# A hybrid DeltaNet and S5 layer: where the S5 output units stand, and when their loads are issued

## The chip, the cores and the metric

The kernel runs on one core of a Trainium2 chip. The core has TensorE (PE, with its weight loads PEld), VectorE (DVE), ScalarE (ACT), GpSimd (POOL) and SyncE (SP), each of which works through its own list of instructions in order, and 16 DMA engines that they share. The metric is the device time of one execution in microseconds, the median over runs.

## The reference

One layer of a streaming encoder, for a prompt of 4096 frames and a running stream of 32 frames, each of width 1024. Cut to what matters:

```
h = rms_norm(x) ;  p = h @ w_in             # q,k,v | a,b | z_dn | u_s5 | z_s5
q,k,v = silu(causal_conv4(p_qkv)) ;  o_dn = gated_delta_rule(q, k, v, g, beta)   # 4 heads of 128
o_dn = rms_norm(o_dn) * silu(z_dn)
y = Re(C x_t) + D u_t ;  x_t = Lbar x_{t-1} + Bbar u_t                           # S5, 32 groups of 16
gy = gelu(y)
o_s5 = gy * sigmoid(gy @ glu_w + glu_b) * silu(z_s5)                             # 512 x 512 matmul
out = rms_norm(x + concat(o_dn, o_s5) @ w_out)
```

The caches and the states at the end are returned too. The frames are independent in all but the convolution, the delta rule (in chunks) and the S5 scan.

## The kernel before, in words

The program is built with a planner: each operation becomes an instruction with a priority (the place at which it was written, unless a priority is given), and the planner sets the order of every engine's list by times that it reckons itself. An engine then keeps to its list; a wait at its head holds all that is behind it. `after(inst, mark)` adds an order between two instructions.

**Phase A** (to some 920 us) does the norm, the projections of u and z, the S5 scan, and the decay tables. `gy = gelu(y)` is left in DRAM as `gy_d`, `silu(z_s5)` as `z5_d`. The largest value of the S5 output is reduced over the partitions by POOL (`allmax`, tile `am_g`); `pow2` (lines 150 to 155, three small DVE instructions) makes of it the power of two `e_gy` by which gy is scaled, and `scales` (L1055) makes the further scales `gs`, `mm`, `hdn`, `ss5` from that. `table(ci)` (L1039) makes one of 33 decay tables: four matmuls into `pt`, one DVE addition into `tdm` (three buffers), four exponentials on ACT, one store to `dm_d`.

**Phase B** interleaves five streams of work in `Drive.run`, which keeps a reckoned time of PE's work: four streams of delta-rule chunks (33 chunks of 128 frames, the sample's among them) go first when they are ready, and the stream `dense` (L1179) fills in between. `dense` does, for each block b of 256 frames, the q, k, v projection (`qkv`, 288 matmuls of 259 columns) and then two **S5 units**. From b = 2 on it first waits until the chunks of block b - 2 have passed their front part. A unit, `s5out(k, j)` (L1435), takes 128 frames of the S5 output: it loads a tile of gy (256 KB, into `gyt`, two buffers) and of z (`zr`, two buffers) by the SP queue, splits gy into two halves `gh` (one buffer; ACT, then DVE, both at line L222 and L223 of a helper), transposes it (four PE instructions, L52), multiplies by the glu weights (12 matmuls of 512 columns, at L48, `pp<-wg,gh`), and finishes by DVE, ACT, DVE, ACT and POOL (L1462 to L1473); the result lies in the buffer of `zr` and is stored by the POOL queue (L1475). There are 32 units of the prompt and one of the sample, (-1, 0). With `LATE = 8`, blocks 1 to 12 are followed by two units each, blocks 13 to 15 by none, and eight units come at the end, behind `c_weights` (L1798), which loads `w_out` through one buffer `xw` in four parts and splits it into `wo`. The units share a ring of three PSUM tiles `pp` with `qkv`.

**Phase C** is `out` (L1820), the output projection of 16 blocks and of the sample; the first seven are the last part of `dense`.

The lines that the change touches most:

```
units = units[:len(units) - LATE]
for b in list(range(1, SP)) + [-1] + list(range(SP, NB)):
    if b > 1:
        yield lambda: {2 * b - 4, 2 * b - 3} <= self.front
    yield from self.qkv(b) if b >= 0 else self.qkv_s()
    for u in units[:2] if b >= 0 else [(-1, 0)]:
        yield from self.s5out(*u)
```

Of the kernel before, what the change touches and what calls it, by code (L numbers as in the profile page):

```python
# [11 lines left out]
ALU = mybir.AluOpType  # L12
# [5 lines left out]
H = 4  # L18
# [3 lines left out]
TS = 32  # L22
# [6 lines left out]
SB = 2  # L29
Z0 = 3  # L30
KS = 4096.0
LATE = 8
SLACK = 1.5


# [44 lines left out]
class Trunk:  # L80
# [168 lines left out]
    def phase_a(self):  # L249
        nc, io = self.nc, self.io  # L250
# [97 lines left out]
        v = nc.vector  # L348
# [3 lines left out]
        v.tensor_single_scalar(mx, mx, 91.0, op=ALU.add)  # L352
        ma = self.allmax(mx, 1, "g")
        self.e_gy = cst.tile([128, 2], F32, name="e_gy")
        self.pow2(ma, self.e_gy[:, 0:1], self.e_gy[:, 1:2])
        self.right.close()
        self.tbl = self.pool(bld, "b_tbl", 3)
        self.pt = self.pool(bld, "b_pt", 2, psum=True)
# [5 lines left out]
        with self.tc.high_priority(offset=-250):  # L364
            for ci in order:
                self.table(ci)

        gcf = self.ngC.rearrange("t h c -> t (h c)")
        mark = self.last_exp
# [669 lines left out]
    def table(self, ci):  # L1039

        nc = self.nc
        gc, c, n = (self.gcr["p"], ci, self.NC) if ci < self.NC else (self.gcr["s"], 0, 1)
        ps = self.pt.tile([128, H, 128], F32, name="pt")
        k = H * n
        for h in range(H):
            p = h * n + c
            nc.tensor.matmul(ps[:, h], self.ident[:k, p:p + 1].to_broadcast([k, 128]), gc, start=True, stop=True)  # L1047
        dm = self.tbl.tile([128, H, 128], F32, name="tdm")
        nc.vector.tensor_tensor(dm, ps, self.low.unsqueeze(1).to_broadcast([128, H, 128]), op=ALU.add)
        for h in range(H):  # L1050
            self.last_exp = nc.scalar.activation(dm[:, h], dm[:, h], AF.Exp, bias=self.ngC[:, h, ci:ci + 1])
            self.after(self.last_exp, self.last_gelu)
        nc.scalar.dma_start(self.dm_d[ci], dm)
# [93 lines left out]
    def phase_b(self):  # L1147
# [30 lines left out]

        def dense():  # L1179
            units = [(k, j) for k in range(NB // 4) for j in range(8)]  # L1180
            late = units[len(units) - LATE:]
            units = units[:len(units) - LATE]
            for b in list(range(1, SP)) + [-1] + list(range(SP, NB)):
                if b > 1:
                    yield lambda: {2 * b - 4, 2 * b - 3} <= self.front
                yield from self.qkv(b) if b >= 0 else self.qkv_s()
                for u in units[:2] if b >= 0 else [(-1, 0)]:
                    yield from self.s5out(*u)
                if b >= 0:
                    units = units[2:]  # L1190
# [206 lines left out]
    def qkv_s(self):  # L1397
# [34 lines left out]
            self.blk[-1, nm] = dst[:, H * i:H * i + H]  # L1432
        yield 0

    def s5out(self, k, j):  # L1435


# [4 lines left out]
        gy, zr, gh = self.rm["gyt"][:, at], self.rm["zr"][:, at], self.rm["gh"][:, 0]  # L1442
        t, m5 = gy, zr
        gy = gy.rearrange("p (o i) -> p o i", o=4)[:, :, :m]
        if k >= 0:
            nc.sync.dma_start(gy, self.gy_d[k].rearrange("o c t -> c o t")[:, :, 128 * j:128 * j + 128])
        else:

            nc.sync.dma_start(gy, self.gys_d.rearrange("o c t -> c o t"))
            g = gh.rearrange("p (o i) -> p o i", o=4)[:, :, :m]  # L1450
            gp.tensor_copy(g.rearrange("p o (i s) -> p o s i", s=8), gy.rearrange("p o (s i) -> p o s i", s=8))
            gp.tensor_copy(gy, g)
        rows = (lambda d: d.rearrange("(i s) d -> s i d", s=8)[j]) if k >= 0 else (lambda d: d)
        nc.sync.dma_start(zr[:m], rows(self.z5_d[k] if k >= 0 else self.z5s_d))
        gh = gh.bitcast(F16).rearrange("p (x o i) -> p x o i", x=2, o=4)[:, :, :, :m]
        self.split(gh[:, 0], gh[:, 1], gy, self.gs)
        pt = self.pb.tile([128, 512], F32, name="pp")[:m]
# [15 lines left out]
        gp.tensor_tensor(m5[:, 1], t, m5[:, 0], op=ALU.subtract)  # L1473
        dst = self.m5_d[k].rearrange("x (i s) d -> x s i d", s=8)[:, j] if k >= 0 else self.m5s_d
        gp.dma_start(dst.rearrange("x t d -> t x d"), m5)  # L1475

    def load_be(self, ci):

# [471 lines left out]
```

## Time and profile before

| what | us |
|---|---|
| median of 3 runs | 2348.45 (2343.35 to 2357.0) |
| the profiled execution, its own time | 2354.65 |
| its span, first to last instruction | 2352.8 |
| PE busy | 2068.0 (88%) |
| DVE / ACT / POOL busy | 1440.2 / 1251.0 / 959.4 |

The span is what the trace covers; the profiled execution's own time is 1.85 us above it, and lies 6.2 us above the median of the runs. Engines work side by side, so their busy times don't add up; a stage is as long as the list of that engine on which the others wait.

### The profile page before, as it was taken

The page shows a single profiled execution, that of the slowest core. Times are in us where ns is not written, and L with a number is a line of the kernel's source. Part 1 is how long each engine was busy: PE and PEld are TensorE (multiplying, and loading weights), DVE is VectorE, ACT ScalarE, POOL GpSimd, SP SyncE. Part 2 cuts the span into 40 slices and gives each one's busy share as a digit, 9 for nine tenths or more (in the row PEclk, how much of TensorE's full clock was granted, in tenths as well). Part 3 has the DMA queues.
Part 4 walks back from the last instruction along what each step waited for, and adds up shares of the span by engine and source line. Part 5 has one row for each costly group of instructions (what it writes and reads, how often), then busy time and mean ns, then how long its engine had stood idle before and what let it go on. Part 6 is the DMA issues. An engine that isn't in the chain of part 4 may idle for free.

```text
span 2352.8 us, 47799 instructions
## 1 busy us (share of the span) xinstructions
PE 2068.0 (88%) x18304; PEld 1492.9 (63%) x18304; DVE 1440.2 (61%) x3289; ACT 1251.0 (53%) x3695; POOL 959.4 (41%) x1444
## 2 busy tenths in 40 slices
PE   4688889888699998698799999989899868999998
PEld 3354677665467554487787778777778755554443
DVE  4685577559466222387687787778777786642223
ACT  5357546543386121376776677667677775431110
POOL 1344225212301012355666666666666675420000
PEclk9899899999899999799899999999999989999999
DMA  6169957765993644323133333322232145455542
GB/s 196 66 175 243 212 116 193 156 54 116 186 235 91 125 114 114 64 59 78 38 79 82 66 80 81 80 62 50 74 82 56 55 146 129 130 165 155 141 139 93
DMA packets 426349, 269.21 MB, mean 114 GB/s; under 512 B 344476, under 2 KB 379384, under 8 KB 425608
## 3 DMA queue, kind: packets, MB, share of 16 engines
q1 hardware_dynamic: 399400, 189.82, 37.1%
q0 software_dynamic: 21968, 67.69, 10.3%
q10 hardware_dynamic: 4752, 8.65, 1.2%
q8 instruction: 143, 2.34, 0.4%
q14 instruction: 86, 0.70, 0.1%
HBM read 102.27 MB, written 86.09 MB: 80 GB/s over the span
## 4 chain that ended last, share of the span: by engine, by line
PE 43%; issue 11%; ACT 7%; DMA 7%; DVE 6%; POOL 4%; SPq 1%; DVEq 0%; POOLq 0%; ACTq 0%
PE pp L48 23%; PE pz L522 9%; PE bk L48 7%; DMA gyt<-gy_d 3%; PE bk L52 2%; DVE acc L1384 2%; ACT jk L1555 2%; DMA dm_d<-tdm 1%; PE pt L1047 1%; DMA hz<-h_d 1%; DVE kn L1667 1%; DMA ab_d<-abt 1%; SPq L1349 1%; ACT acc L1382 1%; ACT br L1642 1%
## 5 line engine op out<-in xcount | busy, mean ns | idle before, releaser
L522 PE MATMUL pz<-wz,hz 128*128 128x512 f16 (+1 forms) x1464 | 385.7, 389 | 27.6 <-DMA hz<-h_d 25.5
L1384 DVE SCALAR_TENSOR_TENSOR acc<-pp,cwu,acc 128x256 f32<-128x256 f32 x540 | 252.9, 477 | 67.4 <-ACT acc L1382 60.6
L48 PEld LDWEIGHTS <-mx 128*128 128x128 f16 (+1 forms) x1584 | 152.3, 98 | 177.2 <-issue 1.6
L522 PEld LDWEIGHTS <-hz 128*128 128x128 f16 (+1 forms) x1464 | 143.4, 99 | 187.3 <-DMA hz<-h_d 33.3
L48 PE MATMUL pp<-h,wk 128*128 128x259 f16 (+1 forms) x1632 | 222.7, 276 | 0.1
L530 PE MATMUL pp<-wa,ht 128*128 128x260 f16 x1536 | 196.3, 284 | 27.1 <-ACT wa L222 10.4
L48 PE MATMUL pp<-h,wq 128*128 128x259 f16 (+1 forms) x1632 | 214.6, 273 | 0.5 <-DVE acc L1384 0.5
L48 PE MATMUL pp<-h,wv 128*128 128x259 f16 (+1 forms) x1632 | 209.9, 272 | 1.0 <-DVE acc L1384 1.0
L48 PE MATMUL po<-wo,mx 128*128 128x512 f16 (+1 forms) x912 | 197.2, 379 | 0.3 <-ACT acc L1219 0.3
L530 PEld LDWEIGHTS <-ht 128*128 128x128 f16 x1536 | 153.7, 101 | 57.1 <-issue 23.9
L48 PEld LDWEIGHTS <-wk 128*128 128x128 f16 x1632 | 156.5, 100 | 35.9 <-issue 8.8
L48 PEld LDWEIGHTS <-wq 128*128 128x128 f16 x1632 | 152.4, 99 | 27.6 <-issue 5.5
L48 PEld LDWEIGHTS <-wv 128*128 128x128 f16 x1632 | 148.5, 98 | 22.6 <-issue 1.6
L48 PE MATMUL pp<-wo,mx 128*128 128x512 f16 x672 | 152.0, 379 | 0.0
L556 POOL DMA_DIRECT2D z_d<-zt x64 | 36.8, 576 | 260.2 <-DVE zt L555 217.4
L1845 ACT ACTIVATE junk<-xt 128x1024 bf16<-128x1024 f32 (+1 forms) x19 | 20.1, 1056 | 176.4 <-issue 92.6
L48 PE MATMUL pp<-wg,gh 128*128 128x512 f16 (+1 forms) x396 | 104.2, 391 | 6.4 <-ACT gh L222 3.4
L555 DVE SCALAR_TENSOR_TENSOR zt<-zt,pz 128x512 f32<-128x512 f32 (+1 forms) x66 | 44.9, 680 | 102.0 <-ACT zt L554 101.3
L1382 ACT ACTIVATE acc<-pp,cwu 128x256 f32<-128x256 f32 x180 | 84.8, 482 | 38.6 <-PE pp L48 38.0
L48 PEld LDWEIGHTS <-a 128*128 128x128 f16 x1320 | 78.2, 98 | 37.3 <-issue 28.3
L1844 DVE SCALAR_TENSOR_TENSOR xt<-po,uo,xt 128x512 f32<-128x512 f32 (+1 forms) x38 | 28.5, 749 | 116.7 <-PE po L48 116.6
L948 POOL DMA_DIRECT2D gy_d<-vv x128 | 67.7, 535 | 78.7 <-ACT vv L943 40.3
(615 smaller groups left out, 5011.1 us busy)
## 6 DMA issues: line engine op xcount, KB each, us to landing
xn<-in_x SPq DMA_DIRECT2D x32, 512.0 KB, 4.5
h_d<-hl POOLq DMA_DIRECT2D x32, 512.0 KB, 5.4
z_d<-zt POOLq DMA_DIRECT2D x64, 256.0 KB, 3.6
xt<-in_x SPq DMA_DIRECT2D x18, 512.0 KB, 4.3
out_y<-xt SPq DMA_DIRECT2D x18, 512.0 KB, 3.6
dm_d<-tdm ACTq DMA_DIRECT2D x33, 256.0 KB, 3.7
dm<-dm_d SPq DMA_DIRECT2D x33, 256.0 KB, 2.9
gy_d<-vv POOLq DMA_DIRECT2D x128, 64.0 KB, 3.9
```

The source lines that it names most:

```text
L48: return self.nc.tensor.matmul(out, lhs, rhs, start=start, stop=stop)
L52: return self.nc.tensor.transpose(out, src, ident)
L522: self.nc.tensor.matmul(ps, a[x][:, c], w[:, y, c], start=c == 0 and x == y == 0, stop=c == K - 1 and x == 1)
L530: self.nc.tensor.matmul(pu[hf][:, :260], ht[x][:, c, :m], self.w_a[:, y, c, 260 * hf:260 * hf + 260], start=c == 0 and x == y == 0, stop=c ...
L555: nc.vector.scalar_tensor_tensor(zt, zt, 1.0, pz, op0=ALU.add, op1=ALU.mult)
L556: nc.gpsimd.dma_start(rows(dst[0][blk]) if blk >= 0 else dst[1], zt)
L948: gp.dma_start(gy[s], gn[16 * s:16 * s + 16, :, :128])
L1047: nc.tensor.matmul(ps[:, h], self.ident[:k, p:p + 1].to_broadcast([k, 128]), gc, start=True, stop=True)
L1382: nc.scalar.activation(acc, ps[:, 0:n], AF.Copy, scale=cw[:, e, 0:1])
L1384: v.scalar_tensor_tensor(acc, ps[:, j:j + n], cw[:, e, j:j + 1], acc, op0=ALU.mult, op1=ALU.add)
L1555: act.activation(junk, src[:, h], AF.Square, accum_out=out[:, h:h + 1])
L1844: v.scalar_tensor_tensor(xt[:m, sl], ps, self.uo[:m], xt[:m, sl], op0=ALU.mult, op1=ALU.add)
```

## The change

It has three parts. `pow2` of the S5 bound, and with it all that is made from it, is written behind the tables, and its first instruction is ordered behind the last table's DVE addition. Of the units, four (`EARLY`) are written between the sample's unit and the wait ahead of block 2, and four instead of eight stay for the end; blocks 1 to 12 keep two each. And the loads move: the first four units (self.nu counts them from 1) load for themselves on SP as before; from the third unit on, each unit ends by issuing the loads of the unit after the next, which uses the same buffers: gy on the POOL queue, behind the unit's own store, and z on the SP queue, where it must wait until that store has landed.

```diff
--- before.py
+++ after.py
@@ -29,7 +29,8 @@
 SB = 2
 Z0 = 3
 KS = 4096.0
-LATE = 8
+LATE = 4
+EARLY = 4
 SLACK = 1.5


@@ -352,7 +353,6 @@
         v.tensor_single_scalar(mx, mx, 91.0, op=ALU.add)
         ma = self.allmax(mx, 1, "g")
         self.e_gy = cst.tile([128, 2], F32, name="e_gy")
-        self.pow2(ma, self.e_gy[:, 0:1], self.e_gy[:, 1:2])
         self.right.close()
         self.tbl = self.pool(bld, "b_tbl", 3)
         self.pt = self.pool(bld, "b_pt", 2, psum=True)
@@ -364,6 +364,8 @@
         with self.tc.high_priority(offset=-250):
             for ci in order:
                 self.table(ci)
+        self.after(v.tensor_single_scalar(ma, ma, 2.0 ** -100, op=ALU.max), self.last_tdm)
+        self.pow2(ma, self.e_gy[:, 0:1], self.e_gy[:, 1:2])

         gcf = self.ngC.rearrange("t h c -> t (h c)")
         mark = self.last_exp
@@ -1046,7 +1048,7 @@
             p = h * n + c
             nc.tensor.matmul(ps[:, h], self.ident[:k, p:p + 1].to_broadcast([k, 128]), gc, start=True, stop=True)
         dm = self.tbl.tile([128, H, 128], F32, name="tdm")
-        nc.vector.tensor_tensor(dm, ps, self.low.unsqueeze(1).to_broadcast([128, H, 128]), op=ALU.add)
+        self.last_tdm = nc.vector.tensor_tensor(dm, ps, self.low.unsqueeze(1).to_broadcast([128, H, 128]), op=ALU.add)
         for h in range(H):
             self.last_exp = nc.scalar.activation(dm[:, h], dm[:, h], AF.Exp, bias=self.ngC[:, h, ci:ci + 1])
             self.after(self.last_exp, self.last_gelu)
@@ -1178,9 +1180,14 @@

         def dense():
             units = [(k, j) for k in range(NB // 4) for j in range(8)]
+            self.useq = units[:2] + [(-1, 0)] + units[2:]
             late = units[len(units) - LATE:]
             units = units[:len(units) - LATE]
             for b in list(range(1, SP)) + [-1] + list(range(SP, NB)):
+                if b == 2:
+                    for u in units[:EARLY]:
+                        yield from self.s5out(*u)
+                    units = units[EARLY:]
                 if b > 1:
                     yield lambda: {2 * b - 4, 2 * b - 3} <= self.front
                 yield from self.qkv(b) if b >= 0 else self.qkv_s()
@@ -1432,6 +1439,14 @@
             self.blk[-1, nm] = dst[:, H * i:H * i + H]
         yield 0

+    def s5load(self, k, j, at, eng):
+        m = 128 if k >= 0 else TS
+        gy = self.rm["gyt"][:, at].rearrange("p (o i) -> p o i", o=4)[:, :, :m]
+        eng.dma_start(gy, self.gy_d[k].rearrange("o c t -> c o t")[:, :, 128 * j:128 * j + 128] if k >= 0 else
+                      self.gys_d.rearrange("o c t -> c o t"))
+        rows = (lambda d: d.rearrange("(i s) d -> s i d", s=8)[j]) if k >= 0 else (lambda d: d)
+        self.nc.sync.dma_start(self.rm["zr"][:m, at], rows(self.z5_d[k] if k >= 0 else self.z5s_d))
+
     def s5out(self, k, j):


@@ -1442,16 +1457,13 @@
         gy, zr, gh = self.rm["gyt"][:, at], self.rm["zr"][:, at], self.rm["gh"][:, 0]
         t, m5 = gy, zr
         gy = gy.rearrange("p (o i) -> p o i", o=4)[:, :, :m]
-        if k >= 0:
-            nc.sync.dma_start(gy, self.gy_d[k].rearrange("o c t -> c o t")[:, :, 128 * j:128 * j + 128])
-        else:
-
-            nc.sync.dma_start(gy, self.gys_d.rearrange("o c t -> c o t"))
+        if self.nu <= 4:
+            self.s5load(k, j, at, nc.sync)
+        if k < 0:
+
             g = gh.rearrange("p (o i) -> p o i", o=4)[:, :, :m]
             gp.tensor_copy(g.rearrange("p o (i s) -> p o s i", s=8), gy.rearrange("p o (s i) -> p o s i", s=8))
             gp.tensor_copy(gy, g)
-        rows = (lambda d: d.rearrange("(i s) d -> s i d", s=8)[j]) if k >= 0 else (lambda d: d)
-        nc.sync.dma_start(zr[:m], rows(self.z5_d[k] if k >= 0 else self.z5s_d))
         gh = gh.bitcast(F16).rearrange("p (x o i) -> p x o i", x=2, o=4)[:, :, :, :m]
         self.split(gh[:, 0], gh[:, 1], gy, self.gs)
         pt = self.pb.tile([128, 512], F32, name="pp")[:m]
@@ -1473,6 +1485,8 @@
         gp.tensor_tensor(m5[:, 1], t, m5[:, 0], op=ALU.subtract)
         dst = self.m5_d[k].rearrange("x (i s) d -> x s i d", s=8)[:, j] if k >= 0 else self.m5s_d
         gp.dma_start(dst.rearrange("x t d -> t x d"), m5)
+        if 2 < self.nu < len(self.useq) - 1:
+            self.s5load(*self.useq[self.nu + 1], at, gp)

     def load_be(self, ci):

```

## Rows read from the trace of the kernel before

**Rows 1.** Windows: us, then busy (x instructions) of PE, PEld, DVE, ACT, POOL, clock, DMA.
```profile
928.00:951.00 23.00, 1.89 (x26) 1.42 (x22) 5.73 (x8) 3.85 (x13) 14.29 (x22) 0.57 0.80 144
951.00:1010.00 59.00, 46.15 (x418) 35.73 (x419) 26.73 (x65) 24.74 (x82) 22.71 (x31) 0.85 0.22 42
...
1178.00:1707.00 529.00, 487.00 (x5646) 421.27 (x5644) 406.29 (x963) 378.95 (x1214) 341.83 (x483) 0.97 0.31 73
1707.00:1891.00 184.00, 169.25 (x2048) 149.68 (x2047) 139.99 (x342) 136.64 (x451) 118.54 (x171) 0.98 0.26 62
1890.00:1946.00 56.00, 36.86 (x327) 25.86 (x325) 48.14 (x75) 38.15 (x97) 38.15 (x41) 0.79 0.52 169
1946.00:1970.00 24.00, 18.48 (x171) 12.36 (x170) 16.55 (x36) 15.06 (x51) 13.38 (x23) 0.86 0.93 187
1970.00:2345.00 375.00, 371.89 (x2142) 183.06 (x2139) 143.22 (x262) 87.10 (x223) 68.80 (x105) 1.00 0.48 132
```

**Rows 2.** The chain that ended last, from 1000 to 1970 us, by line.
```profile
by line: PE pp L48 32.7%; PE bk L48 13.8%; DMA gyt<-gy_d 6.7%; issue 4.9%; DVE acc L1384 3.7%; PE bk L52 3.6%; ACT jk L1555 3.4%; DVE kn L1667 1.6%; ACT br L1642 1.2%; ACT acc L1382 1.2%; ACT gh L222 1.1%; DMA xw<-in_w_out 1.1%; POOL rq_k L
```

**Rows 3.** Waits of ACT, 1010 to 1760 us: total us, times, longest.
```profile
ACT gh L222 <- DMA gyt<-gy_d: 45.3, 11, 6.6
```

**Rows 4.** Timeline around one load of `gyt`: start, us, engine, line [idle before <- releaser].
```profile
1306.98 10.19 SPq L1349 DMA_TRANSPOSE h<-h_d  x1
...
1312.54 1.16 POOL L1473 TENSOR_TENSOR zr<-gyt,zr 128x512 f16<-128x512 f32 x1 [1.81 <-ACT zr L1472]
...
1313.99 0.72 POOL L1475 DMA_DIRECT2D m_d<-zr  x1 [0.30 <-POOL zr L1473]
...
1317.27 0.52 SPq L1446 DMA_DIRECT2D gyt<-gy_d  x1
...
1322.63 0.72 ACT L222 ACTIVATE gh<-gyt,gs 128x512 f16<-128x512 f32 x1 [6.58 <-DMA gyt<-gy_d]
```

**Rows 5.** Windows of 9 us after each of eleven loads: one, and the sum.
```profile
...
1317.27:1326.27 9.00, 4.19 (x46) 3.56 (x44) 3.19 (x7) 3.61 (x9) 1.84 (x2) 0.87 0.52 157
...
sum 99.00, PE 76.64 PEld 67.13 DVE 55.70 ACT 54.73 POOL 46.49; mean PE 6.97 PEld 6.10 DVE 5.06 ACT 4.98 POOL 4.23
```

**Rows 6.** Waits of PE over the whole span, one of its rows.
```profile
PE pt L1047 <- DVE mm L155: 4.2, 1, 4.2
```

**Rows 7.** Timeline of PE: the transposes of the sample's unit.
```profile
951.28 1.04 PE L52 MATMUL pp<-ident,gyt 128*32 128x128 f32 x4 [11.59 <-POOL gyt L1452]
```

**Rows 8.** Timeline of PE: transposes that open an S5 unit (four of many).
```profile
1178.34 0.60 PE L52 MATMUL pp<-ident,gyt 128*128 128x128 f32 x4
...
1707.37 0.27 PE L52 MATMUL pp<-ident,gyt 128*128 128x128 f32 x1
...
1891.60 0.60 PE L52 MATMUL pp<-ident,gyt 128*128 128x128 f32 x4
...
1966.84 0.61 PE L52 MATMUL pp<-ident,gyt 128*128 128x128 f32 x4
```

**Rows 9.** The tail: one unit's matmuls, splits of `w_out`, first output matmuls (first start).
```profile
1893.06 2.75 PE L48 MATMUL pp<-wg,gh 128*128 128x512 f16 x12 [0.86 <-DVE acc L1384]
...
L223 DVE SCALAR_TENSOR_TENSOR wo<-xw,ws_out,wo x8: 1273/1281/2172, 1904.3 to 1943.2; 128x1024 f16<-128x1024 f32 x8
...
L48 PE MATMUL pp<-wo,mx x672: 376/379/380, 1968.7 to 2144.0; 128*128 128x512 f16 x168
```

**Rows 10.** DMA issues: ns min/median/max of the issue, then KB and us to landing.
```profile
L1664 POOL DMA_DIRECT2D vb<-z_d x32: 576/602/628, 1036.1 to 2088.7; - x32
...
L1475 POOL DMA_DIRECT2D m_d<-zr x32: 725/748/836, 881.2 to 1979.5; - x32
...
601.31 1.17 POOL L345 DMA_DIRECT2D out_new_s_re_prompt<-carry_p  x1 [0.29 <-issue]
...
gyt<-gy_d SPq DMA_DIRECT2D x32, 256.0 KB, 4.0
...
vb<-z_d POOLq DMA_DIRECT2D x32, 256.0 KB, 3.0
```

## The prediction

> **What bounds the kernel now.** I read the windows first, cut by stage [rows 1]. From 1970 us to the end PE is busy 371.9 of 375 us: there the time is PE's work, and whatever is taken from PE ahead of it ends the kernel earlier by as much. In the stretch with units (1178 to 1707) PE is busy 487 of 529 us (92.1%), in that without units (1707 to 1891) 169.25 of 184 (92.0%). Three places are emptier: 928 to 951 us (1.89 of 23), 951 to 1010 (46.15 of 59, 78%), 1890 to 1946 (36.86 of 56, 66%); 1946 to 1970 has 18.48 of 24. These are the first chunks and the end of the units, the two places between which the change moves work.
>
> The chain of waits over 1000 to 1970 us puts 6.7% of 970 us, 65 us, on the landing of `gyt` [rows 2]: the loads that the change hastens. The waits of ACT show how they get there: eleven times, once in each pair of units, ACT stands at the split `gh` until the tile lands, 45.3 us in all [rows 3]. The timeline of one of them tells why [rows 4]. POOL is done with the old tile at 1313.70; SP, held by a transposing load of h from 1306.98 for 10.19 us, issues the new load at 1317.27; ACT waits until 1322.63. So the load is already issued when its buffer comes free, a pair ahead of its use: what is late is one instruction of ACT, and what stands behind it. The PE idle time in the eleven windows of 9 us behind the loads is 99 - 76.64 = 22.4 us [rows 5]. That bounds what the waits can cost PE.
>
> **The change part by part.** *The bound.* Removing `pow2` and what follows from the tables' stage takes eleven small DVE instructions (L153 to L155 twice, L1060, L1064, L1065, L1071, L1072) out of the way; PE's one wait that ends at them is 4.2 us [rows 6], and most of it is another DVE instruction between them that stays. Their results are next needed long after the tables. Bounds 0 and -4.2; I take -1 us.
>
> *Four units at the start.* The hole at 928 to 951 stays: PE stands there at the transposes of the sample's unit, 11.59 us of it marked [rows 7], and the new units come behind that one on PE's list, with its load where it was. They can use 951 to 1010. What does a unit cost? Its PE work is 12 matmuls in 2.75 us [rows 9] and transposes of 0.60 [rows 8], 3.35 us, so 13.4 for four. What it costs in the flow I read from the transposes that open a unit [rows 8]: from 1178.34 to 1707.37 lie eight blocks with two units each, 66.1 us a block; from 1707.37 to 1891.60 three blocks with none, 61.4. That is 4.7 us for two units, 2.35 each, 9.4 for four. The stretch from 951 to 1010 has more room than the flow: at 92% busy it would hold 54.3 us of PE work and holds 46.15, 8.2 less. So four units may cost as little as 13.4 - 8.2 = 5.2. At the other end stands the pace of units that follow one another with nothing beside them: from 1891.60 to 1966.84 seven steps [rows 8], 10.75 us each, 43 for four. I take 6, near the lower end, because here chunks and block 2's projection are at hand, as in the flow.
>
> *Four units fewer at the end.* The output projection starts on PE at 1968.7; `wo` has its last split starting at 1943.2 and taking up to 2.17, so it is ready at 1945.4 [rows 9]. Without the last four units PE can begin the output 23.3 us earlier; of that stretch the 5.5 us in which PE idled (24 - 18.48) and about three units' work, 11 us at the lower clock of 0.86 there [rows 1], are saved, 16.5 in all; the fourth ran ahead of `wo`, where its place stays empty. DVE is busy 48.14 of 56 us from 1890 to 1946 and splits `w_out` too, so with less of the units' work on it `wo` comes a little earlier; 1.5 us for that. I take -18. Bounds: -13.4, the units' bare work, and -43, all four at their pace, if `wo` did not bind.
>
> *The loads.* By [rows 4] the new gy load would be issued behind the store, at 1313.99 + 0.72 = 1314.71 rather than at 1317.27. Where SP was free it becomes later by the store's time. So the landing moves by a microsecond or two either way, and ACT's place for `gh` is set anew by the planner, which I can't see. Blocks without units have the same idle share of PE as those with them [rows 1], so the waits seem mostly refilled. Bounds 0 and -22.4; I take -4. The z load waits on SP for the store to land, and behind it stand loads of h, `bl`, `dm` and, at the end, `xw` and the output's transposes; the old z load had the same wait, so I cost this at nothing, and at the store's few us a unit if SP is found late.
>
> *POOL's new issues.* 29 units load gy by POOL. The trace has no such issue; the nearest are a load of the same 256 KB, 0.602 us, the units' own store, 0.748, and a store of many small pieces, 1.17 [rows 10]. I take 0.9, between the store and the last, since gy is read in four pieces a partition: 26 us of POOL. POOL is busy 341.83 of 529 us (65%) in the flow [rows 1], so most of it falls into gaps. Bounds 0 and +34 (29 x 1.17); I take +3.
>
> The Trainium skill speaks against this part: on its page "DMA: Bandwidth & Descriptors", section "Issuing engine by pattern", simple loads belong on Sync, and its specifications give the first byte at about 0.6 us from there and about 1 us from GpSimd. The rows differ: a 256 KB load lands 3.0 us after its issue from POOL and 4.0 after that from SP [rows 10]. An estimate by that page's figures would add 29 x 0.4 = 11.6 us to the sum if every load were waited for.
>
> The sum: -1 + 6 - 18 - 4 + 3 = -14 us against the profiled execution's own 2354.65, thus 2340.7. That execution lies 6.2 us above the median of the runs; taken off the median, 2348.45 - 14 = 2334.
>
> **The rivals.** *The waits go.* If gy lies there whenever `gh` comes, ACT no longer stands 45.3 us, and the 22.4 us of PE idle beside it go rather than 4: 2334 - 18.4 = 2316. For it: the load leaves the queue that the transposing loads hold. Against it: a load that SP did not hold left as soon as its buffer was free, and now leaves behind a store.
>
> *The early units hold block 2* (the slower one). They follow one another, with two buffers for gy and one for `gh`, and `qkv(2)` can't take a PSUM tile before they have had theirs. If they run at the pace of the end, 10.75 us each, less the 8.2 us of room, they cost 43 - 8.2 = 34.8 instead of 6: 2334 + 28.8 = 2363. It turns slower than before once an early unit costs above 6 + 14 = 20 us in four, 5 us each. For it: the pace at the end, where the loads were late too. Against it: at the end there was little else for PE, at the start there is.
>
> *POOL becomes the bound.* If the 29 issues lie on the path of the chunks' fronts, whose steps on POOL others wait for, they cost 26 instead of 3: 2357. The Trainium skill, "SBUF — State Buffer", section "Who interferes with whom", has VectorE and GpSimd hold each other up at a shared port, which would lengthen them; no run here shows such an issue. The rows have POOL 35% free, against it.
>
> *It does nothing of note.* The loads were issued at their buffer's release already, and four units cost the same at both ends, since `wo` binds the end: 2334 + 18 - 6 = 2346.
>
> **How the numbers follow.** About half a per cent, 11.7 us, is what a measurement of this kernel can tell from no change: faster is below 2336.7, slower above 2360.2. Chances: the forecast 0.39 (its own range 2322 to 2345, of which 0.29 lies in faster, 0.10 in the same); the waits go 0.16; early units hold block 2 0.18, slower; POOL 0.12 (0.07 slower, 0.05 the same); nothing of note 0.15, the same. Together faster 0.45, same 0.30, slower 0.25. The range reaches to the rivals on both sides: low, the waits gone and 12 us more at the end than I took (within its bound of -43), 2304; high, the early units at the slow pace with 7 us more on POOL, 2370.
>
> **What would show it.** In the profile after: the units' transposes should stand four times between 951 and some 1010 us, and block 2's projection should end no more than some 6 to 10 us later than it did against them; PE should be full from about 1950 less the gain, with `pp<-wo,mx` starting within a few us of the last split of `wo`; ACT's waits for `gyt` should still be there, in part; POOL's issue of gy should read 0.75 to 1.17 us; the transposes of units in the flow should keep 66 us a block. I am wrong if the early units are some 10 us apart with PE idle between, if the output still starts 20 us behind `wo`, or if the blocks in the flow become longer or shorter by over 2 us, which times eleven would outweigh everything else here.

## The result, and the profile after

The changed kernel takes 2327.44 us (median of four runs, 2324.16 to 2330.99) against 2347.88 for the kernel before: a ratio of 0.9894, interval 0.9868 to 0.9919, 20.4 us off. The forecast was 2334, with 14 us off. The sign was right and the time lies in the forecast's own range, though the change is half as large again; where the time came from was not as forecast.

The profiled execution of the changed kernel has a span of 2322.3 us, 30.5 below the profiled one of before, 10 us more than the medians differ by. So I cut both at marks that every kernel has: the first transposes of a unit (U), the pair of units that opens the eight blocks of [rows 8] and the pair that closes them, the first of the late units, the first matmul with `wo`, and the end. The windows view of the changed kernel (length, then busy time and instructions of PE, PEld, DVE, ACT, POOL, granted clock, DMA):

```profile
859.17:1182.18 323.01, 269.18 (x2731) 204.83 (x2730) 180.33 (x410) 170.29 (x517) 164.64 (x234) 0.90 0.34 79
1182.18:1688.75 506.57, 478.13 (x5626) 415.50 (x5625) 414.91 (x960) 375.54 (x1208) 353.78 (x496) 0.99 0.31 76
1688.75:1873.45 184.70, 171.65 (x2054) 152.56 (x2053) 142.49 (x347) 136.82 (x452) 120.56 (x173) 0.97 0.28 61
1873.45:1935.42 61.97, 38.29 (x355) 28.20 (x354) 48.77 (x82) 42.33 (x117) 43.69 (x51) 0.74 0.67 168
1935.42:2322.30 386.88, 375.50 (x2207) 186.55 (x2205) 147.12 (x276) 91.55 (x240) 70.53 (x114) 0.99 0.49 132
```

The same view of the kernel before, for the two cuts that [rows 1] does not have:

```profile
867.31:1178.34 311.03, 258.37 (x2660) 197.51 (x2658) 166.08 (x395) 161.45 (x505) 147.87 (x216) 0.91 0.33 72
...
1968.71:2352.80 384.09, 373.18 (x2154) 183.88 (x2152) 147.47 (x269) 88.09 (x226) 70.23 (x106) 0.99 0.48 132
```

By stage, after less before: the first chunks 323.0 - 311.0 = +12.0; the eight blocks with units 506.6 - 529.0 = -22.5; blocks 13 to 15, 184.7 - 184.2 = +0.5; the end, from the first late unit to `wo`, 62.0 - 77.1 = -15.1; the output 386.9 - 384.1 = +2.8. From U on that is -22.4. The other 8.1 us lie ahead of U (859.17 instead of 867.31), and one trace can't put them down to the change: a kernel with the same instruction lists, below, has its U at 874.23.

The transposes that open units, on PE's timeline of the changed kernel (start, us, engine, line):

```profile
942.91 1.03 PE L53 MATMUL pp<-ident,gyt 128*32 128x128 f32 x4 [11.58 <-POOL gyt L1466]
944.84 1.12 PE L53 MATMUL pp<-ident,gyt 128*128 128x128 f32 x4
970.27 1.12 PE L53 MATMUL pp<-ident,gyt 128*128 128x128 f32 x4 [4.63 <-DMA gyt<-gy_d]
977.65 0.63 PE L53 MATMUL pp<-ident,gyt 128*128 128x128 f32 x4
987.13 1.12 PE L53 MATMUL pp<-ident,gyt 128*128 128x128 f32 x4 [1.89 <-DMA gyt<-gy_d]
...
1182.18 0.60 PE L53 MATMUL pp<-ident,gyt 128*128 128x128 f32 x4
...
1688.75 0.49 PE L53 MATMUL pp<-ident,gyt 128*128 128x128 f32 x3
...
1873.45 0.49 PE L53 MATMUL pp<-ident,gyt 128*128 128x128 f32 x3
```

The first is the sample's unit, still 11.6 us late as in [rows 7]; the next four are the early units, 7 to 25 us apart, two of them with PE idle for 4.63 and 1.89 us until gy landed. From 1182.18 to 1688.75 a block takes 63.3 us, where [rows 8] gave 66.1; the stretch from there to 1873.45 takes 184.7 us against 184.2. That stretch is not without units, as the prediction had it: the pair whose transposes open it does its matmuls in it. The matmuls with `wg`, 12 a unit, in the two stretches of the kernel before:

```profile
1178.34:1707.37 529.03, 47.23 (x192) 0.97 0.31 73
1707.37:1891.60 184.23, 5.95 (x24) 0.98 0.26 62
```

So eight blocks with 16 units took 529.0 us, and three blocks with two units 184.2. If the blocks are alike, that makes 59.1 us a block and 3.5 a unit, not 61.4 and 2.35. (In the changed kernel the same working gives 60.7 and 1.3.) The eight blocks with two units each became shorter, the other stretch did not. What changed in the eight is in ACT's waits, 1010 to 1760 us:

```profile
ACT gh L223 <- DMA gyt<-gy_d: 8.3, 7, 2.2
```

8.3 us where [rows 3] had 45.3. PE is idle 506.6 - 478.1 = 28.4 us of these blocks instead of 42.0, and its work takes 478.1 us instead of 487.0, 20 matmuls fewer (some 1.7 us at 487.0/5646 each) and at a granted clock of 0.99 instead of 0.97: 13.6 us less of idle time and 8.9 less of work make the 22.5. The timeline around a load of gy, to be read beside [rows 4]:

```profile
1309.48 10.98 SPq L1356 DMA_TRANSPOSE h<-h_d  x1
...
1318.38 0.75 POOL L1487 DMA_DIRECT2D m_d<-zr  x1 [0.30 <-POOL zr L1485]
1319.13 0.77 POOL L1445 DMA_DIRECT2D gyt<-gy_d  x1
...
1325.24 0.32 SPq L1448 DMA_DIRECT2D zr<-z_d  x1
...
1325.91 0.72 ACT L223 ACTIVATE gh<-gyt,gs 128x512 f16<-128x512 f32 x1 [2.24 <-DMA gyt<-gy_d]
```

The transposing load of h holds SP as before, for 10.98 us; POOL issues gy right behind its store, and ACT waits 2.24 us, not 6.58. But the split starts no sooner. The transposes that open the pair, in the kernel before and in the changed one:

```profile
1304.23 0.60 PE L52 MATMUL pp<-ident,gyt 128*128 128x128 f32 x4
```

```profile
1306.88 0.49 PE L53 MATMUL pp<-ident,gyt 128*128 128x128 f32 x3
```

From there to the split are 1322.63 - 1304.23 = 18.4 us before and 1325.91 - 1306.88 = 19.0 after. SP now stands at the load of z instead, for the store to land. The DMA view (bytes, median us from issue to landing) says that the load itself is little faster from POOL, 3.6 us against 4.0 in the kernel before:

```profile
gyt<-gy_d POOLq DMA_DIRECT2D x29, 256.0 KB, 3.6
gyt<-gy_d SPq DMA_DIRECT2D x3, 256.0 KB, 3.1
```

The end of the units in the timeline: the last split of `wo` and the first matmul with it, 4.1 us behind that split's end; in the kernel before 23.3 us [rows 9].

```profile
1927.69 3.62 DVE L224 SCALAR_TENSOR_TENSOR wo<-xw,ws_out,wo 128x1024 f16<-128x1024 f32 x1
...
1935.42 1.06 PE L49 MATMUL pp<-wo,mx 128*128 128x512 f16 x2
```

### The profile page after: what moved, and what is told of

Its sections match the earlier page's. It is cut to its first block, busy times and chain, and to the rows that moved or that the text cites. A ratio compares the mean times of both kernels' runs of the same rounds, so it can differ in the third digit from the quotient of the medians.

```text
span 2322.3 us, 47812 instructions
## 1 busy us (share of the span) xinstructions
PE 2051.7 (88%) x18304; PEld 1488.5 (64%) x18304; DVE 1449.1 (62%) x3290; ACT 1250.9 (54%) x3695; POOL 983.6 (42%) x1473
## 4 chain that ended last, share of the span: by engine, by line
PE 49%; issue 10%; DVE 7%; DMA 6%; ACT 5%; POOL 3%; SPq 1%; DVEq 0%; POOLq 0%; ACTq 0%
PE pp L49 27%; PE pz L524 9%; PE bk L49 8%; PE bk L53 2%; DMA gyt<-gy_d 1%; ACT jk L1569 1%; DVE acc L1391 1%; DMA dm_d<-tdm 1%; PE pt L1049 1%; DMA xw<-in_w_out 1%; DMA hz<-h_d 1%; DMA ab_d<-abt 1%; DVE kn L1681 1%; DVE gyt L1482 1%; PE pp L53 0%
## 5 line engine op out<-in xcount | busy, mean ns | idle before, releaser
L524 PE MATMUL pz<-wz,hz 128*128 128x512 f16 (+1 forms) x1464 | 380.8, 386 | 29.9 <-DMA hz<-h_d 27.9
L49 PE MATMUL pp<-h,wk 128*128 128x259 f16 (+1 forms) x1632 | 217.9, 271 | 0.1
L49 PEld LDWEIGHTS <-wv 128*128 128x128 f16 x1632 | 148.9, 98 | 23.3 <-issue 2.6
L557 DVE SCALAR_TENSOR_TENSOR zt<-zt,pz 128x512 f32<-128x512 f32 (+1 forms) x66 | 44.9, 681 | 101.5 <-ACT zt L556 101.2
```

Of the source, the lines that this page charges most:

```text
L49: return self.nc.tensor.matmul(out, lhs, rhs, start=start, stop=stop)
L524: self.nc.tensor.matmul(ps, a[x][:, c], w[:, y, c], start=c == 0 and x == y == 0, stop=c == K - 1 and x == 1)
L557: nc.vector.scalar_tensor_tensor(zt, zt, 1.0, pz, op0=ALU.add, op1=ALU.mult)
```

## The experiments

Twelve kernels ran, in three groups, each against the kernel before on its own chip; that one had medians of 2360 to 2361 us there, so ratios are compared, not times. In the table each kernel's trace is cut at the marks above; "idle" is PE's idle time in the eight blocks and "clock" the granted clock there; "gyt" is ACT's wait for gyt from 1010 to 1760 us. The stages are of one execution each; the ratios are of all runs.

| kernel | ratio, interval | U to blocks | 8 blocks | idle, clock | blocks 13 to 15 | end | output | gyt |
|---|---|---|---|---|---|---|---|---|
| before | 1 | 311.0 | 529.0 | 42.0, 0.97 | 184.2 | 77.1 | 384.1 | 45.3 |
| changed | 0.9894 (0.9868 to 0.9919) | 323.0 | 506.6 | 28.4, 0.99 | 184.7 | 62.0 | 386.9 | 8.3 |
| bound_only | 0.9977 (0.9953 to 1.0001) | 310.3 | 530.5 | 40.8, 0.97 | 180.5 | 77.7 | 383.5 | 41.0 |
| loads_only | 0.9936 (0.9908 to 0.9964) | 311.1 | 517.0 | 31.5, 0.97 | 186.1 | 79.9 | 386.7 | 12.4 |
| units_only | 1.0029 (1.0007 to 1.0051) | 325.1 | 530.3 | 44.9, 0.97 | 195.0 | 60.7 | 386.5 | 46.8 |
| gy_by_sp | 1.0055 (1.0034 to 1.0076) | 323.7 | 531.2 | 44.8, 0.97 | 195.9 | 64.6 | 386.7 | 47.5 |
| pool_at_use | 0.9898 (0.9873 to 0.9922) | 323.5 | 511.2 | 28.6, 0.98 | 183.7 | 61.9 | 386.8 | 7.3 |
| loads_bound | 0.9928 (0.9901 to 0.9956) | 308.9 | 512.9 | 31.7, 0.98 | 181.3 | 79.3 | 386.7 | 12.7 |
| loads_units | 0.9886 (0.9859 to 0.9913) | 322.3 | 510.4 | 31.0, 0.99 | 186.5 | 54.0 | 388.5 | 9.9 |
| spread | 0.9927 (0.9902 to 0.9952) | 310.4 | 516.5 | 29.5, 0.97 | 197.0 | 61.5 | 388.1 | 13.1 |
| z_pool | 1.0038 (1.0018 to 1.0058) | 329.9 | 529.4 | 37.9, 0.96 | 192.1 | 59.8 | 386.3 | 17.6 |
| two_issues | 0.9927 (0.9899 to 0.9955) | 323.1 | 521.9 | 31.4, 0.97 | 184.2 | 60.3 | 388.7 | 5.1 |
| sample_pool | 0.9938 (0.9913 to 0.9963) | 325.4 | 510.5 | 29.2, 0.99 | 183.8 | 60.5 | 389.7 | 13.9 |
| hole | 0.9927 (0.9901 to 0.9953) | 328.3 | 509.2 | 27.4, 0.98 | 185.2 | 60.8 | 387.7 | 6.0 |

### The three parts alone

**bound_only.**

```diff
-        self.pow2(ma, self.e_gy[:, 0:1], self.e_gy[:, 1:2])
...
                 self.table(ci)
+        self.after(v.tensor_single_scalar(ma, ma, 2.0 ** -100, op=ALU.max), self.last_tdm)
+        self.pow2(ma, self.e_gy[:, 0:1], self.e_gy[:, 1:2])
```

> The kernel before with one part of the change: the bound of S5's output behind the tables. In the changed kernel all of phase A ended 8.4 us earlier (the sample unit's transposes at 942.9 instead of 951.3). Theory one, the bound did that: 8 us off, 2340 at a median of 2348 for the kernel before, and the sample unit's transposes at 943. Theory two, what I took in the prediction: -1 us, 2347, transposes at 950 or later; the 8.4 us then come from the order in which the planner put the rest or from the difference between executions.

Its sample's unit opens at 958.1, later than before; nothing here says that the bound brings phase A forward. The ratio is nothing to 0.5% off, and 1 lies just inside the interval. PE's waits in the tables' stage (560 to 720 us; total, times, longest) say why little comes of it. The kernel before, beside its 4.2 us of [rows 6]:

```profile
PE pt L1047 <- DVE tdm L1049: 16.3, 1, 16.3
...
PE pt L1047 <- DVE mm L153: 1.1, 1, 1.1
```

The changed kernel:

```profile
PE pt L1049 <- DVE tdm L1051: 21.9, 3, 16.4
```

16.3 + 4.2 + 1.1 = 21.6 us have become 21.9 under one name: PE waits for `tdm` as long as it waited for `tdm` and the bound (23.5 us in bound_only itself).

**loads_only.**

```diff
-LATE = 4
-EARLY = 4
+LATE = 8
+EARLY = 0
...
-        self.after(v.tensor_single_scalar(ma, ma, 2.0 ** -100, op=ALU.max), self.last_tdm)
```

(The diff is against the changed kernel; `pow2` stands ahead of the tables again.)

> The kernel before with the loads issued two units ahead alone (gy by POOL behind the store, z by SP); eight units late as before. Theory one, the waits of ACT at the split gh were in PE's path: 60 to 64 us per block with units instead of 66, 20 to 24 us off, about 2326, and the gyt waits of ACT fall from 45 to under 10 us. Theory two, the shorter blocks come from the other order of the units: under 6 us off, 2342 or more. The prediction's own term for loads and issues was -1.

15 us off, and the blocks go from 529.0 to 517.0 with ACT's wait at 12.4: nearer theory one, at two thirds of the size that I expected. The loads make the greater part of the gain by themselves.

**units_only.**

```diff
-LATE = 8
+LATE = 4
+EARLY = 4
...
+                if b == 2:
+                    for u in units[:EARLY]:
+                        yield from self.s5out(*u)
+                    units = units[EARLY:]
```

> The kernel before with four units moved from the end to the first chunks alone, each loading for itself on SP. The prediction's terms: +6 at the start, -18 at the end, -12 in all, 2336. Theory one from the trace after: +12 at the start, -15 at the end, -3 in all, 2345. Theory two, early units hold block 2 when their loads are late (they are not issued ahead here): +20 or more at the start, 2350 or more.

Slower by 0.3%, near theory two in its time but not by its mechanism: the start is 14 us longer, not 20. Two rows of its windows:

```profile
863.33:1188.47 325.14, 268.50 (x2727) 203.11 (x2726) 186.45 (x410) 169.97 (x519) 158.03 (x224) 0.91 0.35 79
...
1718.81:1913.80 194.99, 175.93 (x2071) 156.35 (x2070) 140.87 (x345) 138.88 (x457) 120.45 (x173) 0.96 0.23 59
```

The start costs 325.1 - 311.0 = 14 us, about as much as in the changed kernel, and the end gives 16 back. What makes it slower is blocks 13 to 15, 195.0 us instead of 184.2, with 6.4 us more of PE's work and 4.3 us more in which it idles. With early units that happens where the loads are slow, here, in gy_by_sp and in z_pool; the fast kernels with early units have 183.7 to 186.5. What in these blocks is late the runs do not tell.

### The queue or the place

**gy_by_sp**, the changed kernel with one word of the source different:

```diff
-            self.s5load(*self.useq[self.nu + 1], at, gp)
+            self.s5load(*self.useq[self.nu + 1], at, nc.sync)
```

> The changed kernel with gy's loads at the same place two units ahead, but by SP's queue instead of POOL's. Theory one, the queue is what counts (SP's transposing loads of h hold a load for up to 10 us): the waits of ACT for gyt come back to some 45 us, blocks with units take 66 us, 2345 or more. Theory two, the place in the program is what counts: waits under 10 us, 2327 to 2332.

Theory one: the wait is back, and with it 531.2 us for the blocks:

```profile
ACT gh L223 <- DMA gyt<-gy_d: 47.5, 11, 7.1
```

With the loads written two units ahead but on SP's queue, the kernel is that of units_only in every stage to within 4 us, slower than before by 0.55%.

**pool_at_use** is the other half of the question:

```diff
-        if self.nu <= 4:
-            self.s5load(k, j, at, nc.sync)
+        self.s5load(k, j, at, nc.sync if self.nu <= 4 else gp)
...
-        if 2 < self.nu < len(self.useq) - 1:
-            self.s5load(*self.useq[self.nu + 1], at, gp)
```

> The changed kernel, but each unit from the fifth on writes its own loads at its own start, gy by POOL and z by SP, instead of writing those of the unit after the next at its end. The planner makes the same lists of it on all five engines. Theory one, the place of the loads in the program is nothing and POOL's queue is all: the ratio to the kernel before is that of the changed kernel, 0.989, and the waits of ACT for gyt are under 10 us. Theory two, the place counts: nothing that the lists show could carry it; a ratio above 0.995 would say so, or that one execution differs from another by as much as the whole result.

0.9898, the changed kernel's result, as its lists are the changed kernel's, instruction by instruction on all five engines. "Two units ahead" is nothing to the planner, which had put the loads at their buffer's release in the kernel before too; what counts is that the program gives the load to POOL's queue.

That word does two things, though. It changes the queue on the chip, and it changes the order that the planner gives to the other engines' lists: those of PE, DVE, ACT and POOL in gy_by_sp are not the changed kernel's. The traces say more of how ACT's wait ended. Means over the nine pairs of units behind blocks 4 to 12, in us; "free" is the end of POOL's last reading of the old tile, "between" counts ACT's instructions between the pair's second split and the split that waits:

| kernel | free to issue | issue to split | pair's transposes to split | ACT idle before the split | between (busy us) |
|---|---|---|---|---|---|
| before | 1.4 | 4.6 | 16.6 | 4.4 | 11 (5.2) |
| units_only | 1.7 | 4.5 | 16.9 | 4.8 | 14 (6.1) |
| gy_by_sp | 1.9 | 4.4 | 17.0 | 4.9 | 14 (6.1) |
| changed | 1.4 | 5.0 | 16.7 | 0.8 | 16 (7.1) |
| pool_at_use | 1.4 | 4.9 | 16.7 | 0.7 | 16 (7.1) |
| loads_only | 1.4 | 4.4 | 17.0 | 0.9 | 20 (8.2) |

The load leaves no sooner from POOL than from SP, and the split starts no sooner either. What differs is ACT's list: the planner has put more of ACT's other work ahead of the split, so ACT stands less in front of it. SP held by a transposing load is the smaller part of the old wait. In the kernel before five of the eleven loads were issued 0.8 us or more after their buffer came free, and all eleven together 12.6 us late, beside 45.3 us of waiting; in the changed kernel POOL issues its eleven 15.1 us late, and ACT waits 8.3. One of the loads that SP did not hold, in the kernel before, issued 0.03 us after its buffer came free:

```profile
1090.83 1.16 POOL L1473 TENSOR_TENSOR zr<-gyt,zr 128x512 f16<-128x512 f32 x1 [0.86 <-ACT zr L1472]
...
1092.02 0.37 SPq L1446 DMA_DIRECT2D gyt<-gy_d  x1
...
1097.37 0.72 ACT L222 ACTIVATE gh<-gyt,gs 128x512 f16<-128x512 f32 x1 [4.66 <-DMA gyt<-gy_d]
```

In [rows 4]'s pair ACT does 9 instructions between the two splits in the kernel before and 16 in the changed one. The last ahead of the split that waits, before and after:

```profile
1315.58 0.47 ACT L1382 ACTIVATE acc<-pp,cwu 128x256 f32<-128x256 f32 x1
```

```profile
1323.31 0.36 ACT L1773 CAST p1f<-bk 128x256 f16<-128x256 f32 x1
```

No run has the one queue with the other's lists, so what the queue on the chip is worth by itself, and why the planner orders ACT's list so, stays open.

As a second execution of the changed kernel's lists, pool_at_use shows how far one trace can be trusted:

```profile
874.23:1197.70 323.47, 270.55 (x2731) 205.03 (x2730) 180.61 (x410) 170.49 (x517) 164.05 (x234) 0.89 0.34 79
1197.70:1708.86 511.16, 482.58 (x5627) 417.52 (x5626) 417.04 (x960) 376.85 (x1208) 353.82 (x496) 0.98 0.32 75
```

The stages behind U agree with the changed kernel's to 4.6 us; U itself stands 15.1 us later.

### The parts together

**loads_bound**, **loads_units** and **spread**, in this order and each against the changed kernel:

```diff
-LATE = 4
-EARLY = 4
+LATE = 8
+EARLY = 0
```

```diff
+        self.pow2(ma, self.e_gy[:, 0:1], self.e_gy[:, 1:2])
         self.right.close()
...
-        self.after(v.tensor_single_scalar(ma, ma, 2.0 ** -100, op=ALU.max), self.last_tdm)
-        self.pow2(ma, self.e_gy[:, 0:1], self.e_gy[:, 1:2])
```

```diff
-EARLY = 4
+EARLY = 0
```

> The changed kernel with no units at the start and eight at the end, as before; the bound and the loads stay changed. The trace after has the first chunks 12 us longer with the four units and the end 15 us shorter. Theory one, the move brings these 3 us and little else: a ratio of 0.990 to 0.991. Theory two, the move costs as much as when it stands alone (units_only, +7 us): ratio 0.986. Theory three, the loads and the move help each other: 0.994, as with the loads alone.

> The changed kernel with the bound made ahead of the tables, as before. Theory one, the bound is worth the 5 us that it showed alone, though at the edge of the interval: ratio 0.9915. Theory two, it is worth 1 us or nothing: 0.989 to 0.990.

> The changed kernel with the four moved units two each behind blocks 13 and 14 instead of at the start; four at the end as in the change. Theory one: the first chunks get back 12 us, the end keeps its 15, and a unit in the flow costs 0.9 us (63.3 us a block with two units in the trace after, 61.6 without), so 12 - 4 = 8 us less than the changed kernel, ratio 0.985. Theory two, units so late in the flow push the last blocks and with them the loads of w_out: the end gets later by their full 3.35 us each, 13 us, and the ratio is 0.989 or above.

Without the move 0.9928, between theories one and three; with it 0.9894 and 0.9898. The intervals overlap; by stages the move gives 1469.1 - 1463.1 = 6 us from U on, or 2 against pool_at_use. The same comparison with the bound as before, loads_only 0.9936 against loads_units 0.9886, gives 12 us, and there the intervals overlap by 0.0005. So beside the loads the move is likely worth something, 2 to 12 us; alone it lost. Without the bound 0.9886, so the bound gives nothing here. Spread misses what I expected: the first chunks are short again, but blocks 13 to 15 with two units each behind 13 and 14 take 197.0 us, 11 to 16 more than in the kernels with the same loads and no early units: four units at 2.7 to 3.9 us, not at 0.9, a price that had taken the stretch behind the eight blocks for one without units. The end did not get later, as theory two had it: 61.5 us. Behind the blocks, as before them, a unit costs about its own 3.35 us of PE work.

### What the loads cost POOL, and the hole

**two_issues** and **z_pool**, both in `s5load` of the changed kernel:

```diff
-        eng.dma_start(gy, self.gy_d[k].rearrange("o c t -> c o t")[:, :, 128 * j:128 * j + 128] if k >= 0 else
-                      self.gys_d.rearrange("o c t -> c o t"))
+        src = self.gy_d[k].rearrange("o c t -> c o t")[:, :, 128 * j:128 * j + 128] if k >= 0 else self.gys_d.rearrange("o c t -> c o t")
+        for o in ((0, 2), (2, 4)) if k >= 0 and self.nu > 4 else ((0, 4),):
+            eng.dma_start(gy[:, o[0]:o[1]], src[:, o[0]:o[1]])
```

```diff
-        self.nc.sync.dma_start(self.rm["zr"][:m, at], rows(self.z5_d[k] if k >= 0 else self.z5s_d))
+        eng.dma_start(self.rm["zr"][:m, at], rows(self.z5_d[k] if k >= 0 else self.z5s_d))
```

> The changed kernel with gy loaded by POOL in two halves, so two issues of some 0.77 us a unit instead of one. Theory one, POOL's issues fall into its gaps (65 to 70% busy): +0 to 5 us, ratio 0.989 to 0.992. Theory two, the prediction's rival of POOL as the bound: each issue is paid in full, 29 x 0.77 = 22 us more, ratio 0.998.

> The changed kernel with z's loads on POOL's queue too, behind gy's, where they wait for the unit's store to land (SP stands there 95 to 111 us between 1010 and 1760 us in the changed kernel). Theory one, what PE paid for was ACT's wait for gyt alone: SP set free of z gives nothing, and POOL, which now waits some 2.6 us a unit and issues 29 loads more at 0.6 to 0.8 us, costs 10 us or more: ratio 0.994 or above. Theory two, SP's held queue itself was the cost: blocks with units fall below 63 us and the ratio below 0.986.

The lines view has 56 issues of 0.727 us (minimum, median, maximum in ns) in two_issues, where the changed kernel has 29 of 0.769:

```profile
L1447 POOL DMA_DIRECT2D gyt<-gy_d x56: 722/727/811, 976.0 to 1925.2; - x56
```

The 16 units of the eight blocks have 16 x 0.73 = 11.7 us of POOL more, and the blocks are 11 to 15 us longer than in the two executions of the changed kernel, though ACT waits less than anywhere. That looks as if an issue were paid in full, and is not shown: PE's idle time there is 31.4 us, 3 more than in those two, and the rest is PE's work at a lower granted clock. The eight blocks of spread, without second issues, have nearly as much work at that clock; two_issues, then spread:

```profile
1191.48:1713.37 521.89, 490.53 (x5634) 423.14 (x5631) 418.67 (x960) 377.27 (x1206) 360.69 (x513) 0.97 0.32 74
```

```profile
1182.60:1699.11 516.51, 487.00 (x5630) 423.35 (x5629) 409.33 (x958) 378.13 (x1212) 352.33 (x496) 0.97 0.34 74
```

In the whole 27 x 0.73 = 20 us cost 0.3%, some 7 us, with intervals that overlap. That lies between my two theories, nearer the first. In z_pool POOL stands besides at the unit's store until it has landed:

```profile
POOL zr L1448 <- DMA m_d<-zr: 25.6, 11, 5.6
```

and the whole gain is gone: 529.4 us for the blocks, with ACT's wait at 17.6. Theory one: SP set free of z gives nothing, and the wait for the store now holds POOL. Of the 22.8 us by which these blocks are longer than the changed kernel's, 9.4 are PE's idle time and 13.4 its work, at a granted clock of 0.96.

**sample_pool** and **hole** have gy of the third and fourth unit by POOL, and of the later ones as in the changed kernel; z of the third to the sixth unit too. Hole has the early units ahead of the sample's besides, and writes its loads at their use as pool_at_use does:

```diff
-            self.s5load(k, j, at, nc.sync)
+            self.s5load(k, j, at, nc.sync if self.nu <= 2 else gp)
```

```diff
-                if b == 2:
                 yield from self.qkv(b) if b >= 0 else self.qkv_s()
+                if b < 0:
                     for u in units[:EARLY]:
                         yield from self.s5out(*u)
                     units = units[EARLY:]
```

> The changed kernel with the loads of the sample's unit and of the unit behind it by POOL instead of SP. In the trace after SP issued the sample's load at 938.3, behind a transposing load of 8.2 us, and PE stood 11.6 us at its transposes. Theory one, the same cure as in the blocks: the wait falls below 4 us and 6 to 8 us come off, ratio 0.986. Theory two, PE has nothing else there but the first chunks, which wait for their own loads on SP: the wait only changes its name, ratio 0.989 to 0.990.

> The changed kernel with the four early units ahead of the sample's unit instead of behind it, and the loads of these five units by POOL, so that they can run while PE stands idle from some 922 to 943 us. Theory one, early units cost their full PE time (12 to 14 us in all) because they came behind that hole and the first chunks leave them no room: with the hole used they cost 4 or less, ratio 0.986 or below. Theory two, four units add their time wherever they stand, since what follows them waits behind them: 0.989 to 0.991.

Both miss; neither ratio, 0.9938 and 0.9927, is better than the changed kernel's. In sample_pool PE stands longer at the sample's unit, 22.81 us:

```profile
958.40 1.03 PE L53 MATMUL pp<-ident,gyt 128*32 128x128 f32 x4 [22.81 <-POOL gyt L1466]
```

In hole the wait has changed only its name, from the sample's unit to an early one. Its timeline:

```profile
937.45 0.52 SPq L1492 DMA_DIRECT2D bl<-be_d  x1
...
938.06 9.16 SPq L1356 DMA_TRANSPOSE h<-h_d  x1
...
939.95 0.87 POOL L1445 DMA_DIRECT2D gyt<-gy_d  x1
...
947.52 1.26 POOL L1592 TENSOR_TENSOR br<-bl,dm 128x512 f32<-128x512 f32 x1 [6.47 <-DMA bl<-be_d]
...
950.33 1.09 PE L53 MATMUL pp<-ident,gyt 128*128 128x128 f32 x4 [11.11 <-DMA gyt<-gy_d]
```

POOL comes to gy's load at 939.95, about when PE comes to its hole, and the tile is there only at 950.3, 10.4 us later, where such a load has a median of 3.6. The load of `bl` that SP issued at 937.45 is there at 947.5, 10.1 us later, which is little more than is usual for `bl` in this kernel:

```profile
bl<-be_d SPq DMA_DIRECT2D x32, 256.0 KB, 9.1
```

Both are in flight while SP issues a transposing load of h. Another queue is no cure there: the wait in the hole is for the transfer itself. In sample_pool POOL, held by a wait of 9.15 us for another `bl`, does the second of the sample's copies only at 958.06.

## Why the prediction came out as it did

*The sum came near by luck; the terms were not right.* It had -1 + 6 - 18 - 4 + 3 = -14. Measured by stages, from U on: the bound 0, the early units +12, the loads and POOL's issues together -22.5 (-18 in pool_at_use), the end -15, and the output +2.8, which had no term: -22.4 in one execution and -18.5 in the other, and 20.4 in the medians. The loads gave far more than forecast, the two places of the units less, and that cancelled in part.

*The loads* are the term that was mis-sized: -4 + 3 = -1 taken, -15 measured by loads_only in the whole (-12 to -16 in the blocks without early units, -18 to -22 with them). The step that failed is "blocks without units have the same idle share of PE as those with them, so the waits seem mostly refilled". The blocks called so had a pair of units and one of ACT's waits in them, and an equal idle share does not show refilling. PE's idle time in the eight blocks is 41 to 45 us in every kernel that loads gy by SP, and 27 to 32 in every one that loads it by POOL, but for z_pool. My upper bound of 22.4, the idle time beside the waits [rows 5], was the better number: 13.6 of idle time went from eight of the eleven pairs. The rival "the waits go", which had 0.16, is what happened to the waits; its time, 2316, was not reached, since the early units cost 6 us more than I took and the end gave 3 less.

*The reason behind the term* did not hold. [rows 4] shows SP held by a transposing load, and I took this one load for all eleven; six of them SP issued within 0.3 us of the buffer's release, and ACT waited for those too. What I held against the rival is true: a load by POOL leaves behind a store, 1.0 to 2.5 us after the release in the eleven. And what I could not see, ACT's place for `gh`, is what changed: the tile comes no sooner, and the planner has more work ahead of it. gy_by_sp and pool_at_use show that the queue written in the program makes the difference; that it does so by the order of the lists is read from the traces and not tested by a run. Landing was no part: 3.6 to 3.8 us from POOL, 3.0 to 4.0 from SP in the traces. The Trainium skill, "DMA: Bandwidth & Descriptors", section "Issuing engine by pattern", would have simple loads on Sync; the kernel is faster with its gy loads on POOL, 0.9898 against 1.0055, but by these traces not because a load is there sooner.

*The early units* cost 12 to 14 us instead of 6. Two steps failed. The first is the price in the flow, read from [rows 8] as 9.4 for four: the stretch taken as free of units had two, and with them the same rows give 3.5 a unit, 14 for four. The second is the room: "8.2 us less" than the flow in 951 to 1010 us. PE's idle time from U to the blocks was 311.0 - 258.4 = 52.7 us before and is 323.0 - 269.2 = 53.8 after, so none of it was filled; PE's work grew by 10.8 us (12.2 in pool_at_use), near the four units' own 13.4 [rows 8, 9]. That the first chunks wait there on their own chain, whatever else PE has to do, is likely and not shown. The rival that the units hold block 2 at 34.8 us did not come.

*The end* gave 15 in the changed kernel and 12 to 23 in the others with four late units, where I took 18. The bound by `wo` is right: the first matmul follows its last split by 1.8 to 7.2 us in the ten kernels with four late units, and by 18 to 26 in the four with eight.

*The bound* gave nothing within the interval, -1 taken; the 4.2 us turned into a longer wait for `tdm`.

*POOL's issues* read 0.77 us, not 0.9. What they cost is not measured by itself: the 27 second issues in two_issues cost about 7 us in the whole, with intervals that overlap, so +3 for the first 29 may be too little.

*Of what would show it*: the early transposes, the bound by `wo`, ACT's remaining waits and POOL's issue came as said; the start was to be 6 to 10 us later and is 12. Of the signs of being wrong two came: the early units are 7 to 25 us apart with PE idle for gy between them, and the blocks are 2.2 to 2.8 us shorter than 66, beyond the 2 us that I had named as what would outweigh everything else.

No kernel here beats the changed one by more than its interval; without the bound (0.9886) it is as fast.

## What to carry to other kernels

When an engine waits for a load, take the time of the load's issue and of the waiting instruction from a mark that both kernels have, before the wait is put down to the queue: a wait can vanish though the tile comes no sooner, because the planner has put other work ahead of the waiting instruction. One row of the timeline is not the reason for all of its kind. And a word that changes a load's queue can change the order of every engine's list. Idle time beside a wait is the bound of the gain until something shows that it is refilled, and an equal idle share elsewhere doesn't; look first whether the elsewhere is free of what it is to be compared with. A stretch in which PE idles is not room for more work until a run shows it: four units cost about their own PE time at the start, and four put behind blocks 13 and 14 theirs.

## What the runs showed of the hardware

Two executions of the same instruction lists differed by 15.1 us ahead of their first unit (859.17 and 874.23) and by 3.8 us in all the 1463 us behind it; a single trace's span is not the change's worth. A 256 KB load of gy from POOL took 10.4 us in hole and 6.8 in the row at 1319.13, instead of 3.6; each was in flight while SP issued a transposing load, and in the traces of all kernels with POOL's loads but two_issues the eight such loads with at least 1 us of that beside them, of those whose landing shows, have a median of 6.65 us, the 190 with under 0.3 us one of 3.6. That the transposing load is the reason is not shown.

In the eight blocks the granted clock rose from 0.97 to 0.99 in the changed kernel, and PE's work fell by 8.9 us, two fifths of the 22.5 us there (0.98 and 4.5 us in pool_at_use). In spread, where PE idles as little, 29.5 us, it stayed at 0.97 and the work at 487.0 us. So the fall in work does not simply follow from the fall in idle time, and the part of a single trace's gain that it makes is the less certain one.
